# A narrow load moved ahead of a wide one, and three loads ahead of the opening barrier, in an add and GELU kernel

## The chip, the cores and the metric

The kernel runs on one core of a Trainium2 chip. The metric is the device time of one execution in microseconds (us); smaller is better. Times are given as the median of several runs; the profile is of one further execution, with a span of its own from the first to the last instruction.

## The reference

Two float32 arrays of 1024 x 4096 are added, and the GELU in its tanh form is applied to the sum:

```python
z = x + y
return (0.5 * z * (1 + np.tanh(np.sqrt(2 / np.pi) * (z + 0.044715 * z ** 3)))).astype(np.float32)
```

Each of x, y and the output has 16.8 MB, so 50.3 MB cross between HBM and the core's on-chip memory.

## The kernel before, in words

Every array is seen as 128 partitions with 32,768 columns each (`TOT`). There is one tile `z` of the full width, which takes x, then the sum, then the result, and one tile `y` of half that width (`HALF`, 16,384 columns), which is filled twice. The columns are cut into three transfers for each array: a narrow one of 704 columns (2,816 bytes per partition, 352 KB in all), a wide one of 15,680 columns (62,720 bytes per partition) and a second half of 16,384 columns (65,536 bytes per partition). `rows` maps such a column range to one contiguous block of DRAM, row by row.

Computation goes by 20 chunks of 512 to 2,048 columns. The first chunk has columns 0 to 1,024, so it needs both the narrow and the wide transfer of x and of y. For each chunk:

- `add` (L159) adds x and y, on VectorE (DVE) or, for chunks 7, 8 and 12, on GpSimd (POOL); for some chunks ScalarE (ACT) first copies x to PSUM (`copy`, L152), and the add reads it from there;
- `gelu` (L171) applies the activation on ACT, in place in `z`.

All nine transfers are issued by SyncE (SP), on one DMA queue, in the order of the list `sp`, by `load_x` (L139), `load_y` (L144) and `store` (L148). The first five loads wait for nothing. The sixth, y's second half, overwrites the tile `y` and waits until all adds of the first half are done. Then come the stores: the wide one, the narrow one, and that of the second half. SP runs in order, so an instruction that waits holds all behind it. Four lists (SP, POOL, ACT, DVE) are written out by hand and emitted under a manual schedule; nothing reorders them.

Two functions edit the finished program. `begin_early` takes the first `count` DMA instructions of SP out of the body and puts them at the head of SP's first block, ahead of the barrier by which all engines meet at the start. They may wait for nothing. `wait_late` lets the closing barrier of the engines run before the last store has landed, and has ACT wait for that store at the very end.

In front of the data work, ACT loads its activation table and runs the activation once on a single column (`one`, L199), set by DVE (L198).

Of the kernel before, what the change touches and what calls it, by code (L numbers as in the profile page):

```python
# [8 lines left out]
def begin_early(nc, count):  # L9


    head, body = (b.instructions for b in nc.main_func.blocks[:2])
    SP = mybir.EngineType.SP
    moved = [i for i in body if i.engine == SP and isinstance(i, mybir.InstDMACopy)][:count]
    assert not any(i.sync_info and i.sync_info.on_wait for i in moved)
    assert all(i.regs_accessed() == ((), ()) for i in moved)
    at = next(k for k, i in enumerate(head) if i.engine == SP)
    for k, i in enumerate(moved):
        body.remove(i)
        head.insert(at + k, i)  # L20


def wait_late(nc):

    body, end = (b.instructions for b in nc.main_func.blocks[1:3])
    last = [i for i in body if isinstance(i, mybir.InstDMACopy)][-1]
    (sem,) = [u.id for u in last.sync_info.on_update]
    all_done = end[0]  # L30
    reset = next(i for i in end if isinstance(i, mybir.InstDrain) and i.is_reset_sema)
    at = end.index(reset)
    clear = end[at + 1]
    first, stop = reset.reset_range_start, reset.reset_range_stop
    assert all_done.engine == mybir.EngineType.SP and reset.engine == mybir.EngineType.Pool
    assert isinstance(clear, mybir.InstISA) and clear.engine == mybir.EngineType.Pool
    waits = all_done.sync_info.on_wait
    (its,) = [w for w in waits if w.id == sem]

    end[0] = mybir.InstDrain(  # L40
        name=all_done.name, engine=all_done.engine, debug=all_done.debug, is_reset_sema=False,
        sync_info=mybir.SyncInfo(on_wait=[w for w in waits if w.id != sem], on_update=[]),
    )
    parts = []
    for f, e in ((first, sem), (sem + 1, stop)):
        if f < e:
            nc.gpsimd.sem_clear(range(f, e))
            parts.append(nc.cur_bb.bb.instructions.pop())
    end[at + 1 : at + 2] = parts
    end.append(  # L50
        mybir.InstEventSemaphore(
            name=clear.name, engine=mybir.EngineType.Activation, debug=clear.debug,
            sync_info=mybir.SyncInfo(
                on_wait=[its],
                on_update=[
                    mybir.SyncUpdate(
                        sync_type="semaphore", id=sem, ant_name=its.ant_name,
                        update_mode="sem-sub-imm", update_value=its.wait_value,
                    )
                ],  # L60
            ),
        )
    )
# [3 lines left out]
def kernel(  # L67
# [12 lines left out]
    nc = tc.nc  # L80
# [94 lines left out]
        before = [k for k in copies if k < c and copies[k] < hi and copies[k] + chunks[k] > lo]  # L175
        return [(add, k) for k in before]

    sp = [(load_y, 0), (load_y, 1), (load_x, 0), (load_x, 1), (load_x, 2), (load_y, 2)]
    sp += [(store, i) for i in (1, 0, 2)]
    pool = [(add, c) for c in on_gpsimd]  # L180
    dve = [(add, c) for c in on_vector]
# [30 lines left out]
    ctx.close()  # L212
    tc.close()
    tc.compile()  # L214
    begin_early(nc, 2)
    wait_late(nc)


# [28 lines left out]
```

## Time and profile before

| what | value |
|---|---|
| time, median of 3 runs | 120.1 us (119.8 to 120.74) |
| time of the profiled execution | 120.13 us |
| its span | 118.6 us |
| DVE, ACT, POOL busy | 29.1, 44.1, 13.8 us |
| moved by DMA | 50.33 MB, mean 424 GB/s over the span |
| share of the DMA engines' time taken by packets | 98.6% |
| the two early loads of y, issue to landing | 2.8 us (narrow), 21.2 us (wide) |
| the three loads of x, issue to landing | 21.3 us (narrow), 39.5 us (wide), 58.3 us (second half) |

In the profile, an engine's busy time counts its computing instructions; instructions that issue a DMA belong to the queue side, shown as SPq for SyncE. "Issue to landing" runs from the start of the issuing instruction until the completion of the transfer is seen, and includes the time that the transfer stands behind others in the queue. The share of the DMA engines is the time of all packets, summed, over 16 times the span. Beside the views the trace holds a record of every DMA packet, with its start, its duration and its size: one for each row (partition) of a transfer, and one small one for each engine and transfer that signals the completion.

### The profile page before, as it was taken

How to read it: one execution, taken by the hardware profiler on the slowest of the kernel's cores; microseconds unless marked ns; L12 is line 12 of the kernel's file. 1: busy time of each engine (PE TensorE's matmuls, PEld its weight loads, DVE VectorE, ACT ScalarE, POOL GpSimd, SP SyncE). 2: the span in 40 equal slices, each digit the busy share in tenths (PEclk: the TensorE clock that was granted, in tenths of full speed). 3: DMA queues.
4: the chain of work that ended last, by engine and by line, in shares of the span. 5: the costliest groups of instructions: out<-in, count | busy, mean ns of one | idle time of the engine just before them, and what ended most of it. 6: DMA issues, size and time to landing. Idle time of an engine off the chain costs nothing.

```text
span 118.6 us, 119 instructions
## 1 busy us (share of the span) xinstructions
DVE 29.1 (25%) x18; ACT 44.1 (37%) x30; POOL 13.8 (12%) x7
## 2 busy tenths in 40 slices
DVE  0000000000000099994000000009999920000000
ACT  5000000000000196792059999904799980000000
POOL 0000000000000029970000000009500000000000
DMA  9779977999789888988899889977997789988891
GB/s 460 338 338 571 444 338 338 460 571 444 338 360 656 354 354 376 663 376 354 354 597 464 354 354 508 552 338 338 529 486 338 338 385 517 619 354 354 354 663 44
DMA packets 1296, 50.33 MB, mean 424 GB/s; under 512 B 144, under 2 KB 144, under 8 KB 528
## 3 DMA queue, kind: packets, MB, share of 16 engines
q1 hardware_dynamic: 1296, 50.33, 98.6%
HBM read 33.55 MB, written 16.78 MB: 424 GB/s over the span
## 4 chain that ended last, share of the span: by engine, by line
DMA 55%; DVE 14%; ACT 10%; DVEq 1%; ACTq 0%; SPq 0%; issue 0%
DMA z<-in_x_dram 33%; DMA y<-in_y_dram 21%; DVE z L159 14%; ACT z L171 10%; DVEq L214 1%; ACTq L214 0%; SPq L139 0%; DVEq L159 0%; SPq L144 0%
## 5 line engine op out<-in xcount | busy, mean ns | idle before, releaser
L171 ACT ACTIVATE z<-z 128x2048 f32<-128x2048 f32 (+3 forms) x20 | 29.7, 1555 | 5.6 <-DVE z L159 5.6
L152 ACT COPY ps<-z 128x2048 f32<-128x2048 f32 (+2 forms) x8 | 13.0, 1654 | 46.6 <-DMA z<-in_x_dram 44.9
L159 DVE TENSOR_TENSOR z<-z,y 128x2048 f32<-128x2048 f32 (+2 forms) x9 | 13.6, 1574 | 39.9 <-DMA z<-in_x_dram 39.9
L159 DVE TENSOR_TENSOR z<-ps,y 128x2048 f32<-128x2048 f32 (+2 forms) x8 | 15.6, 2016 | 25.4 <-DMA y<-in_y_dram 25.4
L159 POOL TENSOR_TENSOR z<-z,y 128x2048 f32<-128x2048 f32 x3 | 13.6, 4538 | 70.6 <-DVE z L159 43.3
L199 ACT ACT_TABLE_LOAD x1 | 1.3, 1283 | 1.3 <-PEq L231 1.3
L198 DVE MEMSET one<- 128x1 f32 x1 | 0.1, 59 | 1.3 <-PEq L231 1.3
L199 ACT ACTIVATE one<-one 128x1 f32<-128x1 f32 x1 | 0.2, 202 | 0.0
L231 POOL MEMSET const-float32-0.0<- 128x1 f32 x1 | 0.1, 99 | 0.2 <-issue 0.2
L231 POOL MEMSET const-bfloat16-1.0<- 128x1 bf16 x1 | 0.1, 101 | 0.0
L231 POOL MEMSET const-uint8-127<- 128x1 uint8 x1 | 0.1, 101 | 0.0
L231 POOL MEMSET const-float32-1.0<- 128x1 f32 x1 | 0.1, 98 | 0.0
## 6 DMA issues: line engine op xcount, KB each, us to landing
y<-in_y_dram SPq DMA_DIRECT2D x1, 7840.0 KB, 21.2
z<-in_x_dram SPq DMA_DIRECT2D x1, 7840.0 KB, 39.5
out_dram<-z SPq DMA_DIRECT2D x1, 7840.0 KB, 21.4
y<-in_y_dram SPq DMA_DIRECT2D x1, 352.0 KB, 2.8
z<-in_x_dram SPq DMA_DIRECT2D x1, 352.0 KB, 21.3
out_dram<-z SPq DMA_DIRECT2D x1, 352.0 KB, 21.9
z<-in_x_dram SPq DMA_DIRECT2D x1, 58.3
y<-in_y_dram SPq DMA_DIRECT2D x1, 25.2
```

The lines of the kernel that those rows point to most:

```text
L152: nc.scalar.copy(out=in_psum(c), in_=zt[:, a:b])
L159: ins = eng.tensor_add(out=zt[:, a:b], in0=first, in1=yt[:, o : o + b - a])
L171: nc.scalar.activation(out=zt[:, a:b], in_=zt[:, a:b], func=act.Gelu_apprx_tanh)
L198: nc.vector.memset(one[:, :1], 0.0)
L199: nc.scalar.activation(out=one[:, :1], in_=one[:, :1], func=act.Gelu_apprx_tanh)
L214: tc.compile()
L231: nc = _bacc.Bacc("TRN2", target_bir_lowering=False, num_devices=1)
```

## The change

The narrow load of x moves from the third to the second place in SP's list, ahead of y's wide load. The count given to `begin_early` goes from 2 to 3, so the narrow load of y, the narrow load of x and the wide load of y, in this order, stand ahead of the opening barrier. The other instructions of all engines keep their order. The semaphores of the two loads that change places are numbered in the new order, and the waits follow.

```diff
-    sp = [(load_y, 0), (load_y, 1), (load_x, 0), (load_x, 1), (load_x, 2), (load_y, 2)]
+    sp = [(load_y, 0), (load_x, 0), (load_y, 1), (load_x, 1), (load_x, 2), (load_y, 2)]
     sp += [(store, i) for i in (1, 0, 2)]
...
-    begin_early(nc, 2)
+    begin_early(nc, 3)
     wait_late(nc)
```

## Prediction

> **What bounds the kernel now.** I read the busy shares first, then the DMA lines, then the queue's issues, and last the chain of waits, to see whether anything but data movement ever sets the pace.
>
> ```profile
> DVE 29.1 (25%) x18; ACT 44.1 (37%) x30; POOL 13.8 (12%) x7
> ...
> DMA packets 1296, 50.33 MB, mean 424 GB/s; under 512 B 144, under 2 KB 144, under 8 KB 528
> ...
> q1 hardware_dynamic: 1296, 50.33, 98.6%
> ```
>
> No engine is busy for even half of the span, while the one DMA queue's packets take 98.6% of what 16 DMA engines have in 118.6 us. At most 1.4%, or 1.7 us, of DMA time is idle. The order of two loads can only win from that, or from packets that run slower than usual.
>
> ```profile
> core 0: us, DVE busy (x) ACT busy (x) POOL busy (x), PEclk, DMA share, GB/s
> 0.00:1.00 1.00, 0.00 (x0) 0.00 (x0) 0.20 (x4) 1.00 0.01 3
> 1.00:97.00 96.00, 29.11 (x18) 43.59 (x30) 13.57 (x3) 1.00 1.01 433
> ```
>
> These are two windows of the span. In the first microsecond nothing moves (the first issue is still on its way). From then on the engines are full, at 433 GB/s; a packet is credited whole to the window in which it starts, so shares slightly over 1 are possible.
>
> The trace's own records of DMA packets, one for each row of a transfer, say the rest. A 2,816 byte row of a narrow transfer takes 0.112 us on its DMA engine, a 62,720 byte row 2.314 us, a 65,536 byte row 2.418 us. Each of the 16 DMA engines carries 8 rows of each of nine transfers (three of each width): 8 x (3 x 0.112 + 3 x 2.314 + 3 x 2.418) = 116.26 us. The first packet starts at 0.99 us, the last ends at 118.25 and its landing is seen at 118.59. So the bare work would end at 117.25 on an engine without any gap, and 1.00 us is spent otherwise on the last engine. The records show where: the engines start one after another over 0.47 us (0.99 to 1.46); the rows of the first narrow load cost 1.15 us per engine instead of 0.90 (first ones up to 0.57 us each); the first two rounds of y's wide load cost 0.20 and 0.04 us too much (mean 2.514 and 2.358 instead of 2.314); one engine has 0.21 us of gap right behind the narrow load of x, before its first wide row of x.
>
> ```profile
> start us, us, engine line op out<-in xcount [idle before <-releaser]
> 0.00 0.85 SPq L144 DMA_DIRECT2D y<-in_y_dram  x2
> ...
> 1.25 1.28 ACT L199 ACT_TABLE_LOAD   x1 [1.25 <-PEq L231]
> 1.25 1.34 SPq L139 DMA_DIRECT2D z<-in_x_dram  x3
> 1.32 0.06 DVE L198 MEMSET one<- 128x1 f32 x1 [1.32 <-PEq L231]
> ...
> 41.29 2.36 DVE L159 TENSOR_TENSOR z<-z,y 128x1024 f32<-128x1024 f32 x2 [39.91 <-DMA z<-in_x_dram]
> ...
> 54.70 0.33 SPq L144 DMA_DIRECT2D y<-in_y_dram  x1
> ```
>
> All five opening loads are issued by 2.59 us, far ahead of what the DMA engines have done. Engines that compute first do anything with data at 41.2 us, when x's first wide load has landed: chunk 0 (columns 0 to 1024) needs both narrow loads and both wide ones.
>
> ```profile
> 54.70 25.20 DMA y<-in_y_dram
> ...
> 84.61 11.86 ACT z L171 x7
> 96.47 0.52 ACTq L214
> 96.98 0.52 ACT z L171
> ```
>
> The chain of waits makes it look as if the compute between y's last landing (79.90) and the last store's issue (97.53) were on the path. It barely is not: the last store's first packet starts at 98.37, while the narrow store's last packet ends at 98.93 on the latest engine. That engine has 0.56 us in hand; earlier ones wait for up to 0.19 us.
>
> **The change, part by part.**
>
> *Issue.* SP issues y narrow, x narrow, y wide ahead of the barrier instead of y narrow and y wide. An issue of a narrow load took 0.37 (y) and 0.33 us (x), of a wide one 0.42 to 0.46. With the 0.05 us between two, y's wide load is issued at 0.42 + 0.33 + 0.05 = 0.80 instead of 0.42, and SP comes to the barrier 0.38 us later. The barrier's release goes from 1.2 to 1.6 us, and with it the ACT table load, the two small instructions on `one` and POOL's, all 0.38 later. Their cover is the idle time until 41.2 us; the price without it would be the whole 0.38. Wide x, which is now first behind the barrier, is issued at 1.25 + 0.38 = 1.63, where it is issued now (1.25 + 0.33 + 0.05). Nothing later on SP moves.
>
> *Does the queue run dry?* Issue to first packet took 0.99 us on the first engine and 1.46 on the last. The narrow load of x, issued at 0.42, is there at 1.41 to 1.88; the first load's packets run until 2.05 to 2.42, so it is at least 0.5 us early. Wide y, issued at 0.80, is there at 1.79 to 2.26, and the two narrow loads end at 2.05 + 0.90 = 2.95 to 3.32: about 1.1 us early. Cost nothing; without the cover, 0.38 us.
>
> *The moved rows.* The narrow load of x took 0.903 us per engine in mid-queue (0.902 at 20.8 to 22.2 us). At the head its rows follow those of y directly. Bounds: 0.90 as in mid-queue, 1.15 as y's first, cold ones, so +0.00 to +0.25. Its rows come 1 us after the start, when y's own last rows are already at 0.112, but their source is untouched so far; I take +0.10. The slow first rounds of wide y (0.24 us) may go, now that the engines have run longer and the issues of wide x are past, or stay: -0.24 to 0.00, and I take 0.00, since the rows are as new to it as before. The gap of 0.21 us on one engine stood behind the narrow load in mid-queue. That engine is among the last at the end (the two last end at 118.25, most others near 117.75). Without the narrow load there it should go: -0.21 to 0.00; I take -0.15, since another engine ends as late.
>
> A rule of the Trainium skill, page "DMA: Bandwidth & Descriptors", in the anatomy of a DMA, speaks against the change: each DMA has a fixed cost of about 2.0 us beside its bytes over 436 GB/s. If that were serial, a narrow load at the head, with nothing in front to hide it, would put some 2.8 us (an estimate by that page: 2.0 + 0.36 MB over 436 GB/s) ahead of wide y, and the sum would be some 1.9 us more than with the 0.90 us it took in mid-queue, 122.0. The trace disagrees: y's narrow load lands at 2.77 us, but wide y's first packet starts at 2.05, right behind the narrow load's packet, without waiting for the landing.
>
> *Downstream.* The queue carries the same four loads before the middle of the kernel, so wide x lands where it did, at 41.16, give or take the terms above. y's second half is issued at 54.70, once the adds of the first half are done; x's second half keeps the engines until 59.5 to 60.1, and with 1.46 us from issue to packet there are 3.3 us to spare. The last store's 0.56 us does not change either, since its issue and the drain of the other stores both follow y's last landing.
>
> *Sum.* +0.10 + 0.00 - 0.15 = -0.05 us against the profiled execution's span of 118.63 and its own time of 120.13 (1.5 us lie around the span): 120.08, which is also the median's size (120.1). The bounds of the terms add up to -0.45 and +0.25: 119.7 to 120.4. The three runs spread from 119.8 to 120.74, so the same kernel's runs already differ more than that. I forecast 120.1.
>
> **The rivals.**
>
> *Slower: wide y's slow first round stays slow.* Its first 16 rows took 2.514 us in the mean (up to 2.971) instead of 2.314. If the engines leave two narrow loads in closer step than one, and the rows disturb each other as in that round, for all of y's eight rounds, 7 x 0.20 = 1.4 us are added: 121.5. It decides from the sixth slow round on (6 x 0.20 = 1.2 us, 1%). For it: the slow rows are those that all engines start within 0.4 us. Against: in the next rounds it is 0.044 and 0.004, though the engines keep their phases. Chance 0.06.
>
> *Slower by less: the head is cold.* x's narrow rows cost the full 1.15 us, the gap moves to another engine, and wide y's rounds are slow as well: 120.13 + 0.25 = 120.4, or 120.5 with the 0.1 by which engines could be further apart. The cold first rows speak for it, the fast last ones against. Chance 0.2, within no change.
>
> *Faster: the start-up losses all go.* -0.24 and -0.21 without the cold term: 119.7. More would need the DMA engines to exceed 27.1 GB/s each, which no wide row did (62,720 bytes in 2.314 us); the floor is 0.99 + 116.26 + 0.34 for the landing + 1.5 around = 119.1, and that is still only 0.9% below. Chance 0.24 for about 119.7; below 1% there is room only by the spread of the runs, 0.03.
>
> *The queue runs dry,* if a third DMA ahead of the barrier is late: with 1.1 us of cover, wide y would have to come over twice as late as the first load did. A milder form is that wide y waits until the narrow loads have landed: y's landed 0.35 us after its last packet, so 0.35 us more, up to 0.5 with the engines' spread, 120.6. Against both: wide y did not wait for the landing of the load ahead of it (first packet 2.05, landing 2.77). Chance 0.03.
>
> **How the numbers follow.** Forecast (within 0.2 us of 120.1) 0.44; cold head 0.20; start-up losses gone 0.24 + 0.03; slow rounds 0.06; dry queue 0.03. About 1% (1.2 us) is what a measurement of this kernel can tell from no change: beyond it lie only the slow rounds (0.06) above and the tail of the gone losses (0.03) below, which leaves 0.91. The range holds the forecast and both small cases, widened by the spread of the runs: 119.4 to 120.9.
>
> **What would show it.** Right: the SP issues at 0.00, 0.42 and 0.80, then wide x at about 1.63; ACT's table load at about 1.63; DMA share again about 98.6%; wide x's landing within 0.4 us of 41.16 and the first add right behind; y's second half issued near 54.7; span 118.2 to 119.0. Wrong: windows between 1 and 5 us with a DMA share visibly lower, wide rows of y above 2.32 us beyond the second round, or wide x landing beyond 42 us. An end later than 119.8 with the first landings unchanged would mean that the compute behind y's second half ran out of its 0.56 us, which I hold to be unaffected.

## The result and the profile after

The changed kernel is slower: 121.63 us (median of 5 runs, 121.36 to 122.35) against 120.19 us (5 runs, 119.8 to 120.74). The ratio is 1.0126, 95% interval 1.0078 to 1.0174. The forecast was 120.1 us, no change, within 119.4 to 120.9. Ratios here leave out runs more than 1.5% above the fastest of the same kernel (five of e5's twelve); over all sets the kernel before took 121.3 to 122.5 us in 13 of its 97 runs, and no trace shows where those lose their time.

The profiled execution took 121.54 us with a span of 120.1, 1.4 to 1.5 us more than before. First its page, busy time of the engines, DMA packets, and the share of the queue:

```profile
DVE 29.1 (24%) x18; ACT 44.1 (37%) x30; POOL 13.8 (11%) x7
...
DMA packets 1296, 50.33 MB, mean 419 GB/s; under 512 B 144, under 2 KB 144, under 8 KB 528
...
q1 hardware_dynamic: 1296, 50.33, 97.9%
```

The engines compute for as long as before and the same bytes move in as many packets. The queue's share fell from 98.6% to 97.9%: there is more idle time of DMA engines. Next the timeline, where columns are start, length, engine, line and operation:

```profile
0.00 0.38 SPq L144 DMA_DIRECT2D y<-in_y_dram  x1
...
0.43 0.42 SPq L139 DMA_DIRECT2D z<-in_x_dram  x1
0.90 0.43 SPq L144 DMA_DIRECT2D y<-in_y_dram  x1
1.74 1.28 ACT L199 ACT_TABLE_LOAD   x1 [1.74 <-PEq L231]
1.74 0.86 SPq L139 DMA_DIRECT2D z<-in_x_dram  x2
...
42.62 2.36 DVE L159 TENSOR_TENSOR z<-z,y 128x1024 f32<-128x1024 f32 x2 [40.76 <-DMA z<-in_x_dram]
...
56.05 0.33 SPq L144 DMA_DIRECT2D y<-in_y_dram  x1
```

The issues stand where the prediction put them, give or take 0.1 us, and wide x is still issued well ahead of need. Yet the first add starts at 42.62 instead of 41.29, and y's second half is issued 1.34 us later. The pages' DMA issues (KB, then us from issue to landing) narrow it down, the wide loads before and then the loads after:

```profile
y<-in_y_dram SPq DMA_DIRECT2D x1, 7840.0 KB, 21.2
z<-in_x_dram SPq DMA_DIRECT2D x1, 7840.0 KB, 39.5
```

```profile
y<-in_y_dram SPq DMA_DIRECT2D x1, 7840.0 KB, 23.1
z<-in_x_dram SPq DMA_DIRECT2D x1, 7840.0 KB, 40.8
...
y<-in_y_dram SPq DMA_DIRECT2D x1, 352.0 KB, 2.7
z<-in_x_dram SPq DMA_DIRECT2D x1, 352.0 KB, 3.8
```

Before, wide y was issued at 0.42 and landed 21.2 us later, at 21.6. Now it lands at 0.90 + 23.1 = 24.0. Narrow x, now ahead of it, is good for 0.9 of these 2.4 us; about 1.5 us are new, about as much as the kernel lost. The chain of waits from there on is the old one, 1.35 us later at the issue of y's second half and 1.25 us later after its landing:

```profile
56.05 25.11 DMA y<-in_y_dram
...
85.86 11.86 ACT z L171 x7
97.72 0.52 ACTq L214
98.23 0.52 ACT z L171
```

So the loss arises in the first microseconds. The records of DMA packets show it in parts. A round is the n-th row of a transfer on each of the 16 DMA engines. The table has means over the 16 engines, in us: time beyond the usual one of a row (0.112, 2.314 us), or without any row:

| | before | after |
|---|---|---|
| rows of narrow y slower | 0.25 | 0.14 |
| rows of narrow x slower | 0.01 | 0.20 |
| rows of wide y slower (nearly all in rounds 1 and 2) | 0.28 | 0.67 |
| rows of wide x slower | 0.00 | 0.09 |
| no row in work, from 1.0 to 5.2 us | 0.10 | 0.30 |
| sum | 0.64 | 1.40 |
| last engine done with wide x at | 40.81 | 42.18 |

From 3.0 to 4.0 us only 12.7 engines in the mean have a row in work (9.7 at 3.0); the rest have finished narrow x and have no row in work. Wide y's first rows start at 3.07 to 4.08 us, one engine after another, and six of the 16 take 3.16 to 3.59 us instead of 2.31. The loss per engine is 0.76 us in the mean, but unevenly spread: one engine is 1.37 us later than the latest one was before. Every landing waits for the last engine, so its 1.37 us, not the mean, go to the end. In the profiled executions of the kernels below the time is 79.2 to 79.4 us after the last engine's end of wide x, with two exceptions at 79.7 and 79.8: nearly all that differs among them is done by then. The other engines show it once more at the end. The last store can only be issued 1.25 us later (98.78 instead of 97.53), and most engines, having been less late, stand idle ahead of its first row, for up to 1.03 us and 0.46 us in the mean (0.04 before).

### The profile page after: what moved, and what is told of

It reads as the page before. It is cut to its first block, busy times and chain, and to the rows that moved or that the text cites. A ratio compares the mean times of both kernels' runs of the same rounds, so it can differ in the third digit from the quotient of the medians.

```text
span 120.1 us, 119 instructions
## 1 busy us (share of the span) xinstructions
DVE 29.1 (24%) x18; ACT 44.1 (37%) x30; POOL 13.8 (11%) x7
## 3 DMA queue, kind: packets, MB, share of 16 engines
q1 hardware_dynamic: 1296, 50.33, 97.9%
## 4 chain that ended last, share of the span: by engine, by line
DMA 55%; DVE 14%; ACT 10%; DVEq 1%; ACTq 0%; issue 0%; SPq 0%
DMA z<-in_x_dram 34%; DMA y<-in_y_dram 21%; DVE z L159 14%; ACT z L171 10%; DVEq L214 1%; ACTq L214 0%; DVEq L159 0%; SPq L144 0%
## 6 DMA issues: line engine op xcount, KB each, us to landing
y<-in_y_dram SPq DMA_DIRECT2D x1, 7840.0 KB, 23.1
```

## The experiments

Three theories stood at the start. *Late supply*: wide y, as third transfer, is not there in time. *Crowding*: the issues of wide x and of x's second half, at 1.7 to 2.6 us, disturb wide y's first rows. *Cold x*: narrow x is slow so early. Later ones are named where they arose. "Start-up loss" in the table is the sum of the rows above without wide x: rows of the loads up to wide y, and of narrow x, that are too slow, and no row in work. It and the last engine's end are those of the profiled execution, which need not be the median run. Medians come from several sets of runs; ratios are against runs of the kernel before in the same set.

| kernel | loads in the queue up to wide y, in columns | start-up loss | last engine ends wide x | median us (runs) | ratio [95% interval] |
|---|---|---|---|---|---|
| before | y 704, wide y | 0.64 | 40.81 | 120.19 (5) | 1 |
| changed | y 704, x 704, wide y | 1.31 | 42.18 | 121.63 (5) | 1.0126 [1.0078, 1.0174] |
| e1 | the same, wide y behind the barrier | 1.29 | 41.42 | 122.13 (7) | 1.0161 [1.0132, 1.0190] |
| e2 | y 704, wide y (three ahead of the barrier) | 0.81 | 41.41 | 120.17 (12) | 1.0000 [0.9979, 1.0021] |
| e3 | y 1408, x 1408, wide y | 0.91 | 40.94 | 120.22 (12) | 0.9998 [0.9978, 1.0017] |
| e4 | wide y | 0.78 | 40.78 | 120.16 (10) | 0.9986 [0.9965, 1.0007] |
| e5 | as changed, wide x issued at 4.0 us | 1.36 | 43.01 | 121.80 (12) | 1.0073 [1.0034, 1.0113] |
| e6 | y 1408, wide y | 0.73 | 40.71 | 120.06 (10) | 0.9974 [0.9940, 1.0007] |
| e7 | y 352, y 352, wide y | 2.02 | 42.93 | 122.20 (4) | 1.0123 [1.0060, 1.0186] |
| e8 | y 704, the same y again, wide y | 1.87 | 42.85 | 122.21 (4) | 1.0119 [1.0054, 1.0183] |
| e9 | y 704 in two rows each, wide y | 0.71 | 41.50 | 120.49 (10) | 0.9998 [0.9961, 1.0035] |
| e12 | y 256, y 1152, wide y | 0.87 | 41.12 | 120.51 (10) | 1.0020 [0.9985, 1.0054] |
| e13 | y 1152, y 256, wide y | 1.57 | 42.50 | 121.81 (4) | 1.0126 [1.0062, 1.0191] |
| e14 | y 704, wide y behind the barrier | 0.91 | 41.06 | 121.78 (4) | 1.0150 [1.0064, 1.0236] |
| e15 | y 256, wide y | 1.08 | 41.55 | 120.71 (10) | 1.0031 [0.9996, 1.0065] |

**Which part of the change does it?** e1 is the new order with two loads ahead of the barrier, e2 the old order with three.

```diff
# e1, against the changed kernel
-    begin_early(nc, 3)
+    begin_early(nc, 2)
# e2, against the kernel before
-    begin_early(nc, 2)
+    begin_early(nc, 3)
```

> The new order with only two loads ahead of the barrier (narrow y, narrow x; wide y behind it). Late supply (wide y, as third transfer, is not there when the engines have done two narrow loads): wide y is issued some 0.35 us later than in the changed kernel (1.25 instead of 0.90), the engines idle that much longer around 3 to 4.5 us, 121.7 to 122.2 us. Crowding (the issues of x's two large loads disturb wide y's first rows): wide y is followed by x's loads as closely as before, 121.4 to 121.8. If three loads ahead of the barrier were the cause: 120.2.

> The old order with three loads ahead of the barrier. Late supply, crowding, and cold x alike: wide y again starts right behind one narrow load at 2.05 us, 120.0 to 120.4. If three loads ahead of the barrier were the cause by themselves: 121.6.

e1 is as slow (one of its seven runs, the profiled one, took 120.77, the others 121.96 to 122.57), e2 is the kernel before. So the order does it alone. Putting three loads ahead of the barrier costs nothing. But e1 also spoke against late supply as I had it: wide y was issued 0.36 us later than in the changed kernel, yet its first rows start at 3.13 to 3.91 us, no later (in the profile of that quick run, the only one kept).

**Crowding.** In e5 wide x waits until narrow x has landed.

```diff
+        ins = nc.sync.dma_start(out=zt[:, a:b], in_=rows(x, a, b))
+        if i == 1:
+            tc.add_manual_dep(ins.ins, xdma[0].name, ...)
```

> The changed kernel, but wide x (and with it x's second half) is issued only when narrow x has landed, at about 4.2 us instead of 1.74. Late supply: nothing changes, engines still short of rows from 3.0 to 4.1 us, 121.4 to 121.8. Crowding: the dip and the slow first rows of wide y go, 120.2 to 120.5.

Three of its runs took 120.1 to 120.6, nine 121.7 to 122.4; the profiled one is of the nine. Wide x is issued at 4.03 there, and still 13 of 16 engines have a row in work from 3.3 to 3.8 us, and a first row of wide y takes 3.67 us. The issues of wide x are not needed for the loss; crowding fell as its cause. Whether they make the loss more frequent is open: three quick runs of twelve here, none of five in the changed kernel.

**Cold x.** e3 makes the narrow transfers twice as wide, e8 lets the second load read the narrow block of y, which was just read.

```diff
# e3
-    blocks = [(704, 16384), (16384, TOT), (0, 704)]
+    blocks = [(1408, 16384), (16384, TOT), (0, 1408)]
-    xloads = [704, 15680, HALF]
+    xloads = [1408, 14976, HALF]
...
# e8
-        nc.sync.dma_start(out=zt[:, a:b], in_=rows(x, a, b))
+        nc.sync.dma_start(out=zt[:, a:b], in_=rows(y if i == 0 else x, a, b))
```

> The changed kernel with narrow transfers of 1408 columns and wide ones of 14976, in x, y and the output. Late supply: the two narrow loads now keep the engines until some 4.8 us, wide y is there long before, no dip in active engines, 120.1 to 120.4. Crowding: x's issues are past by then as well, 120.1 to 120.4. Cold x (narrow rows of x at the start are slow because nothing of x was read): still slow, 121.4 or more.

> The changed kernel, but the second load takes the narrow block of y once more instead of that of x (so these columns hold twice y). Cold x: its rows are quick and the dip goes, 120.1 to 120.5. Late third transfer, and many short rows ahead: as the changed kernel, 121.4 to 121.9.

e3 has the changed order and costs nothing; e8 has no x at the head and costs all. Cold x fell, and the time at which wide y's turn comes (5.0 us in e3) began to matter.

**Count, rows or time?** e6 is the old order with 1408 columns, e7 cuts narrow y into two loads, e9 leaves it one load but with two rows for each partition.

```diff
# e7
-    yloads = [704, 15680, HALF]
+    yloads = [352, 352, 15680, HALF]
...
-    begin_early(nc, 2)
+    begin_early(nc, 3)
# e9, load_y(0)
...
+            src = y.rearrange("n d -> (n d)")[at : at + P * b].rearrange("(h p c) -> p h c", h=2, p=P)
+            nc.sync.dma_start(out=yt[:, 0:b].rearrange("p (h c) -> p h c", h=2), in_=src)
```

> The kernel before with narrow transfers of 1408 columns and wide ones of 14976: wide y comes to the engines at about 3 us, as in the changed kernel, but as the second transfer and behind 8 rows per engine. Late third transfer, and many short rows ahead: no dip, 120.1 to 120.4. A slow stretch of time from 3 to 4 us, whatever the transfers: a dip there, 121 or more.

> The kernel before, with narrow y cut into two loads of 352 columns, both ahead of wide y and all three ahead of the barrier: bytes ahead of wide y as before, but 16 rows per engine and wide y as third transfer. Late third transfer: wide y at 3.1 us or later, idle from 2.1 us, 121.5 to 122.5. Many short rows ahead: 121 to 122. Cold x (no row of x at the head): 120.2. A slow stretch from 3 to 4 us: 120.2.

> The kernel before, with narrow y still one load of 704 columns, but of two rows of 1408 bytes for each partition (from another place in the same block of y, so the sums of these columns are of other elements): 16 rows per engine ahead of wide y, which is the second transfer. Late third transfer: no dip, 120.1 to 120.4. Many short rows ahead: engines dip once those are done, 121 to 122. Cold x: 120.2.

In e6 wide y begins at 3.2 to 3.5 us, just when the changed kernel starves, and nothing is lost: it is no matter of the clock. e7 and e9 put the same bytes and the same 16 rows per engine ahead of wide y; as two loads they cost 1.2%, as one nothing, give or take 0.35%. It is no matter of how many rows. Only the number of loads, or what lies right ahead of wide y, was left.

**When does a transfer come to the engines?** e10 has six loads of y, five of them so short that the engines run dry after each. e4 has wide y first, e11 issues it from ScalarE's queue.

```diff
# e10
-    yloads = [704, 15680, HALF]
+    yloads = [128, 128, 128, 128, 192, 15680, HALF]
...
# e4, against the changed kernel
-    sp = [(load_y, 0), (load_x, 0), (load_y, 1), ...
+    sp = [(load_y, 1), (load_y, 0), (load_x, 0), ...
# e11, emitted ahead of everything else
+        eng = nc.scalar if i == 1 else nc.sync
...
```

> The kernel before with the 704 columns of narrow y cut into five loads (four of 128 columns, one of 192), wide y sixth, all six ahead of the barrier. The rows are so short that the engines are done with each load before the next comes, so first packets show when transfers come to the engines. Transfers served one by one: the second to sixth begin about 1 us apart (2, 3, 4, 5, 6 us) though they are issued 0.45 us apart; wide y at about 6, 123 to 125 us. Issue plus a fixed 1.0 to 1.5 us: they begin 0.45 us apart, wide y at 3.3 to 3.8 us, 121 to 122.

> The changed kernel with wide y first, then the two narrow loads, all three ahead of the barrier. Late third transfer: its lateness lies beneath some 18 us of wide rows, no dip, 119.7 to 120.3; the cold first rows are wide ones, so 0.3 us less than before may show. Three loads ahead of the barrier as a cost of its own: 121 or more.

> The changed kernel, but wide y is issued by ScalarE, right behind the barrier, on a queue of its own; SP has the two narrow loads ahead of the barrier, wide x and the rest behind it. One queue serves its transfers one by one: wide y is the first of ScalarE's and comes about 1.0 to 1.5 us after its issue at 1.3, before the narrow rows end, no dip, 120.0 to 120.5. Third transfer late whatever the queue: a dip from 3 to 4 us again, 121.4 to 122.

e10 was run once (122.04 us). Its issues are 0.47 us apart, and the first rows of the six loads start at 1.01, 1.49, 1.98, 2.44, 2.92 and 3.39 us: each 1.0 to 1.1 us after its issue, the third like the first. Late supply in its plain form fell: transfers do come on time. What is late are the rows of wide y themselves: in e10 they start at 3.39 to 4.13 us, and their ends correspond to an undisturbed start at 4.25 to 5.00. In e4, with nothing ahead, the first rows start at 1.01 to 2.00 us and end as if started at 1.57 to 2.04. There this delay takes the place of the slow rows of narrow y and the sum stays as before, evenly over the engines. e11 (122.01 us, 9 runs, ratio 1.0100 [1.0055, 1.0146]) did not put the question to wide y: wide x, as SP's third transfer, came to the engines ahead of ScalarE's wide y, and now it was late, with 9.5 engines at 3.5 us and first rows of up to 3.79 us. So the late load need not be one of y.

Read so, the first rows of a wide load come to their usual pace 0.6 to 1.0 us after the load's first row has started in e4 (1.01 to 1.57 and 2.04) and 0.9 to 1.6 us after it in e10 (3.39 to 4.25 and 5.00), and this costs nothing only where other rows fill the time. "Preparation" is only a name for this delay; no record shows what it consists of. The new theory: wide y is prepared while the load right ahead of it is worked on, and not earlier, so this load must be long enough.

**The test of it.** e12 and e13 have the same bytes, the same three loads and the same issue times; only the two loads ahead of wide y change places.

```diff
# both: narrow transfers of 1408, wide ones of 14976, three loads of y ahead of the barrier
...
# e12
+    yloads = [256, 1152, 14976, HALF]
# e13
+    yloads = [1152, 256, 14976, HALF]
# e14, against the kernel before
-    begin_early(nc, 2)
+    begin_early(nc, 1)
```

> The kernel before with narrow transfers of 1408 columns and narrow y cut into two loads, of 256 and then of 1152 columns; wide y is the third transfer, issued at 0.9 us, and reached at about 3.1 us as in the changed kernel. One transfer of read-ahead (a transfer's first rows are prepared only while the one right ahead of it is worked on): 1152 columns give 1.5 us of cover, no dip, 120.1 to 120.5. Third transfer late: a dip at 3 to 4 us as in the changed kernel, 121.4 to 122.2.

> The same, with the load of 1152 columns first and that of 256 right ahead of wide y: the same bytes, count, issue times and arrival. One transfer of read-ahead: only 0.3 us of cover, wide y's first rows are late on many engines, 121.5 to 122.5. Third transfer late: as the other order, 121.4 to 122.2. If only the time from issue to need counted (2.2 us in both): no dip in either.

> The kernel before with only narrow y ahead of the barrier: wide y is still the second transfer, but issued at about 0.85 instead of 0.42. One transfer of read-ahead: it is prepared from its arrival at 1.85 on, 0.4 us later, with some 0.45 us of cover left, 120.3 to 121.2. Third transfer late: it is the second, 120.1 to 120.4.

The pages' DMA issues (KB, us to landing), e12 first, then e13:

```profile
y<-in_y_dram SPq DMA_DIRECT2D x1, 7488.0 KB, 21.2
...
y<-in_y_dram SPq DMA_DIRECT2D x1, 576.0 KB, 3.8
y<-in_y_dram SPq DMA_DIRECT2D x1, 128.0 KB, 2.1
```

```profile
y<-in_y_dram SPq DMA_DIRECT2D x1, 7488.0 KB, 22.6
...
y<-in_y_dram SPq DMA_DIRECT2D x1, 576.0 KB, 3.7
y<-in_y_dram SPq DMA_DIRECT2D x1, 128.0 KB, 3.6
```

Issued at the same time, wide y lands 1.4 us later where the short load is right ahead of it, and the first add that waits for wide x starts at 42.96 instead of 41.56. In e12 all 16 engines have a row in work from 2.7 us on and wide y's first rows are 0.08 us slow in the mean; in e13 engines fall to 12.7 at 3.4 us, first rows are 0.43 us slow in the mean, and the slowest takes 3.2 us instead of 2.2. With ten runs of 120.34 to 120.94 against four of 121.58 to 122.08 the two do not overlap. (e12 is not quite free: its median is 0.4 us above the 120.09 of the kernel before in this set, e13's 1.7 us.) A load of 1152 columns right ahead of wide y hides its start even in third place; one of 256 there does not, though the one before it has 1152.

e14 shows that the issue time is not free either: wide y in second place, issued at 0.79 instead of 0.42, so that it comes at 1.8 us with the narrow rows ending at 2.4 to 2.8. Its profiled run took 120.29, the other three 121.61 to 122.75; the profile of the quick one already has first rows 0.40 us slow in the mean.

**Is it cover alone, and long rows alone?** e15 leaves wide y in second place but with only 256 columns ahead; e16 puts a load of 2048 columns of y in third place, ahead of the rest.

```diff
# e15: blocks and loads of 256 and 16128 columns
# e16, against the changed kernel
-    yloads = [704, 15680, HALF]
+    yloads = [704, 2048, 13632, HALF]
...
```

> The kernel before with narrow transfers of 256 columns and wide ones of 16128: wide y is the second transfer, issued at 0.42 us, and the load ahead of it is worked off in about 0.5 us. Cover alone: it is late as in the changed kernel, rows from 2.3 us on, engines idle from 1.6, 121 to 122. Place in the queue: the second is prepared together with the first, the first rows' delay is paid once, 120.0 to 120.5.

> The changed kernel with wide y cut into a load of 2048 columns, third in the queue and ahead of the barrier, and one of 13632 behind the barrier. Any third load that touches the new part of y right behind a short one is late: its rows (0.3 us each) start late, 121.2 to 122.2. Only the longest rows are late: 120.1 to 120.6.

e15 lies between: engines are short of rows from 1.4 to 2.6 us (7.0 at 1.5), but its ratio is 1.0031 with an interval that includes no change, where the changed kernel's is 1.0126. So cover is not the whole rule; in second place less of it is needed, or a lack costs less. e16 took 122.17 us (4 runs, ratio 1.0111 [1.0048, 1.0174]): its rows of 0.31 us are late as well, those that start first taking up to 1.46 us, and only about 9 engines have a row in work from 3.3 to 3.8. It isn't the long rows.

Left open is what begins the preparation: the start of the load ahead, or the landing of the one before that (in e13 that is at 3.2 to 3.7 us, in e12 at about 2.1; both readings fit the times of the kernels). Neither holds for every engine by itself: in e13 one begins wide y at 3.20 us with a row of the usual 2.21. Nor do the runs show why some engines wait for 0.3 us and others for 1.5.

## Why the prediction was wrong, step by step

- *What bounds the kernel*: right. The DMA engines do, compute follows y's second landing with the same 18.5 us from that landing to the last store's first packet, and the 0.56 us in hand there was not what gave way: on the latest engine it is still 0.56 (first packet at 99.62, that engine's last row of the narrow store done at 100.18).
- *Issue*: right, small. The barrier's release came at 1.7 instead of 1.6 us and nothing waited for it; e2 confirms that this is free.
- *Does the queue run dry?* This is the step that failed. It took 0.99 to 1.46 us from issue to first packet, measured on a narrow load in an empty queue, as the time at which wide y would be ready, and concluded that it was 1.1 us early and cost nothing. e10 shows that the figure holds for the first row of all six of its loads. But other rows of the load start later than that or run slowly, and how much of it is hidden depends on the load right ahead (e12 against e13). Cost 0.00, measured +0.20 of idle time and +0.39 of slow rows in the mean.
- *The moved rows*: narrow x's +0.10 became +0.20, within its bounds of 0.25; narrow y's rows gave back 0.11. The slow first rounds of wide y, for which I took 0.00 between -0.24 and 0.00, went the other way. The bounds shut out a loss, on the ground that these rows were as new as before. They were; but the load ahead of them was another one, and it kept the engines for 0.9 us behind another short load.
- *The gap on one engine*, -0.15: the spread among engines grew instead. The mean loss of 0.76 became 1.37 on the last engine. The sum had no term for spread at all, though the last engine makes the landing.
- *Downstream*: what the prediction calls the drain of the other stores follows each engine's own rows, not y's last landing. With engines 1.5 us apart at the end of wide x (40.70 to 42.18; 0.6 before), the early ones drain first and wait for the last store, as shown above.
- *The rivals*: the dry queue was named, at a chance of 0.03 and for 0.5 us. The engines did run dry between 3 and 4 us, but the price was that of the slowest engine. "Slow first round stays slow" forecast 121.5, near the time only by chance: round one lost 0.49 us instead of 0.20 and round two 0.14 instead of 0.04, and later ones 0.02 or less each.
- *The rule of a fixed cost* in the prediction gave 122.0, near the time too, but not for its reason. That section of the Trainium skill, page "DMA: Bandwidth & Descriptors", gives the fit for DMAs that GpSimd issues, and these are SyncE's. And wide y did not wait for a landing: its first row starts at 3.07 us, while narrow x lands at 4.2.
- *What would show it wrong*: wide x's landing beyond 42 us did (42.5). Rows of y above 2.32 us beyond the second round did so weakly: 16 instead of the 5 that the kernel before has already. The windows with a lower DMA share did not, because a packet of 2.3 us is credited whole to where it starts (from 1 to 97 us both kernels read 433 GB/s). Only the packets' records show idle engines at this scale.

The Trainium skill, page "HBM Reference", section Latency, gives 0.2 us for an access on average and 2 us at high load. The first rows of wide y took up to 1.3 us beyond their usual duration in the changed kernel, no more than the latter; that it is this latency no run here shows.

## What to carry to other kernels

In a queue that is never empty, the order of loads is not free at its head. In this kernel it cost nothing to put the long load first, or second and issued early, and little or nothing to put it third behind a load of 1152 columns or more. Two loads of 704 or 352 columns in front of it, or one of 256 right ahead of it in third place, did cost (e3, e4 and e6 cost nothing, e12 about 0.4 us; the changed order, e7 and e13 over 1%, and e14, with the long load second but issued 0.37 us later, in three runs of four). When a transfer is moved, cost its first rows on the slowest DMA engine, not its arrival and not the mean. None of the versions beat the kernel before beyond the noise (e6 comes nearest, 0.9974 with an interval up to 1.0007), and its start-up loss of 0.64 us is the lowest in these profiles.

## What the runs showed of the hardware

- A transfer's first row starts 1.0 to 1.1 us after its issue, whether it is the first or the fifth on its queue (e10), but the first rows of wide y needed 1.6 to 2.0 us from issue to an undisturbed start with nothing ahead (e4), and behind two short loads the last engine came to it only 4.3 us after the issue (changed kernel: issued at 0.90, as if started at 5.20), though those loads' rows had all ended by 3.89.
- Once an engine is late it stays late: the last engine's 1.37 us at the end of wide x was 1.42 us at the end of the last store (119.67 against 118.25). The records don't name the engines, but if each row is followed to the one that starts as it ends, 16 chains come out with 24 rows of 65,536 bytes each, so none took over rows of another.
- Two loads of 352 columns instead of one of 704 cost over 1% (e7: ratio 1.0123, medians 122.20 and 120.28), through the wide load behind them.
